# Two layers of a hybrid diffusion backbone: some output-projection rows take the second token set behind the norm, and three gate/up accumulators run k-tile by k-tile

## The chip, the cores and the metric

The kernel runs on one core of a Trainium2 chip. Its engines work side by side and wait for each other by semaphores: TensorE (PE, the matrix products, with its weight loads PEld), VectorE (DVE), ScalarE (ACT), GpSimd (POOL) and SyncE (SP, whose queue issues the DMA transfers). Each engine takes its own instructions strictly in the order in which they stand. The metric is the device time of one execution in microseconds, as the median of several runs.

## The reference

Two layers work on 512 latent tokens ("LAT") and 256 context tokens ("CTX") of width 1024. The second layer reads the context but updates only the latent tokens.

```python
for l in range(DEPTH):                       # DEPTH = 2
    need_ctx = l < DEPTH - 1
    h = modulate(rms_norm(x, g_mix[l]), mx[:, 0], mx[:, 1])
    # w_in, then three mixers: latent attention (MLA), neighbourhood attention, gated DeltaNet
    ...
    x = x + mx[:, 2] * (jnp.concatenate([mla_o, na_o, dn_o], axis=-1) @ w_out[l])
    h = modulate(rms_norm(x, g_ffn[l]), mx[:, 3], mx[:, 4])
    x = x + mx[:, 5] * swiglu(h, w_gate[l], w_up[l], w_down[l])
    if need_ctx:
        # the same two steps for ctx, with mc, mla_c, na_c, dn_c
        ...
return rms_norm(x, g_final)
```

## The kernel before

**Products.** Each fp32 matrix is split into a high and a low part in TensorE's fp32r type, and a product is made of three: high x high, high x low, low x high (`mm3`, and `gemm` at L343 to L350, which runs over k-tiles). All activations lie transposed: 128 channels on the partitions, tokens as columns. A matmul takes at most 512 columns, so LAT is one matmul and CTX a matmul of 256.

**Weights.** `wtiles` (L206 to L218) loads a weight tile by SP into `wr` (two buffers), casts it on ScalarE into the high part (`wh`, or `kh` for a slot of its own), and subtracts on GpSimd to get the low part (`wl`, `kl`). `wr` is free again when the subtraction has read it; `wh` and `wl` have two buffers each.

**Output projection** (L1240 to L1298). The token sets of layer 0 are LAT and CTX. In layer 1 there is only LAT; it is one set for the first part and two halves of 256 columns (`HALVES`) for the second. The first part (`acc_o`) runs over eight row tiles m: a weight tile of `w_out` (128 x 768), then for each token set 18 matmuls (six k-tiles, three products each) over the DeltaNet and neighbourhood outputs. VectorE adds the result into `xT` (L1273). The second part (`acc_o2`) takes the remaining two k-tiles, those of latent attention, with six matmuls for each m, and loops over token sets first and then m. As soon as the first set has all its m, `rstd_of` (L268 to L291) makes its norm: ScalarE squares (`nacc`, `nsq`), VectorE and GpSimd add them up, two PE products with a matrix of ones (`ms`) sum over partitions, and ScalarE makes Ln and Exp (`nrs`). The second set's `acc_o2` follows and is PE's work during that chain.

**Accumulators.** PSUM has 8 banks. In layer 0 `acc_l` is one bank of 512 columns, `acc_c` one of 256, and `acc_b` gives three of 512 and two of 256. `acc_c` serves the context's `acc_o`, and its `acc_o2` of every third m.

**Gate and up projection** (L1305 to L1345). `norm_mod` (L293 to L306) makes one k-tile of the normed input: VectorE multiplies (`nt`, two buffers), ScalarE adds the shift and rounds (`fh`), VectorE makes the low part (`fl`). The first tiles of `w_gu` begin on the first token set while its k-tiles come in (`first`, two accumulators; each a `gemm` of its own), and take the second token set later. The FFN's accumulators `acc_gu` (1024 columns, four buffers) reuse the banks of the output projection as these come free.

**Order.** A tile scheduler puts each engine's instructions in order from its own estimate of the times. So the order of the code says only what depends on what, and a small edit moves rows far behind it.

Of the kernel before, what the change touches and what calls it, by code (L numbers as in the profile page):

```python
# [17 lines left out]
P = 128  # L18
D = 1024
KD = D // P  # L20
# [5 lines left out]
LAT = slice(0, TL)  # L26
HALVES = (slice(0, TL // 2), slice(TL // 2, TL))
CTX = slice(TL, T)
# [18 lines left out]
INV = ((4, 3), (4, 3))  # L47
WV = ((6,), (23,))
MR = 2
MLA_ENG = ["GGVVGVGGV", "GGVGVVVGV"]  # L50
TILE_KV, TILE_QL, TILE_AB, TILE_K, TILE_V, TILE_Q, TILE_NK, TILE_NQ, TILE_Z = 0, 1, 3, 4, 8, 12, 16, 18, 20
HS = [slice(h * P, (h + 1) * P) for h in range(4)]
# [48 lines left out]


def mm(nc, out, lhsT, rhs, start=True, stop=True):
    nc.tensor.matmul(out, lhsT, rhs, start=start, stop=stop)  # L104


def mm3(nc, out, l, r, start=True, stop=True):
# [18 lines left out]
def emit(ctx, tc, a, out, dbg=None):  # L126
    nc = tc.nc
# [213 lines left out]
    def gemm(acc, wh, wl, xh, xl, sts, c0=0):  # L341

        nk = len(xh)  # L343
        for st in sts:
            for k in range(nk):
                w = slice(k * P, (k + 1) * P)
                o = acc[:, st.start - c0:st.stop - c0]
                mm(nc, o, wh[:, w], xh[k][:, st], k == 0, False)
                mm(nc, o, wh[:, w], xl[k][:, st], False, False)
                mm(nc, o, wl[:, w], xh[k][:, st], False, k == nk - 1)  # L350


    es_x = ExitStack()
# [9 lines left out]
def layer(tc, nc, a, l, es_x, xT, env, nx):  # L363
# [900 lines left out]
    def out_proj(nm, m, st_, s, w, mh, ml):  # L1264
        n = st_.stop - st_.start
        if nm == "acc_o":
            acc = (acc_l if st_ == LAT else acc_c)(nm)
        elif st_ in HALVES:
            acc = acc_l(nm)[:, 0:n] if m % 8 in (0, 1) else acc_b(nm, 512)[:, 0:n] if m % 8 < 5 else acc_c(nm) if m % 8 == 5 else acc_b(nm, n)
        else:  # L1270
            acc = (acc_l if st_ == LAT else acc_c)(nm) if m % (BO[n] + 1) == 0 else acc_b(nm, n)
        gemm(acc, *w, mh, ml, (st_,), st_.start)
        stt(out=xT[:, m, st_], in0=acc, scalar=mod[l][:, 2, m, s:s + 1], in1=xT[:, m, st_], op0=ALU.mult, op1=ALU.add)  # L1273
# [8 lines left out]
            tt(out=mxl[:, :, tok], in0=qT[:, :, tok], in1=mxh[:, :, tok].bitcast(F32), op=ALU.subtract)  # L1282
    m6 = [(mxh[:, i], mxl[:, i]) for i in range(4)] + [load_split(mp, i) for i in (2, 3)]
    m0 = load_split(mp, 0)
    for m in range(KD):
        w = wtiles(a["w_out"][l, m], 6 * P)
        for s, st_ in enumerate(sts):
            out_proj("acc_o", m, st_, s, w, *zip(*m6))

    wb = [wtiles(a["w_out2"][l, i], 1024, mp, 2) for i in range(2)]  # L1290
    segs, es_r = sts if need_ctx else HALVES, ExitStack()
    sb = pool(es_r, f"sb_fn{l}", 2, side=A_)
    for st_ in segs:
        for m in range(KD):
            c = (m % 4) * 2 * P
            out_proj("acc_o2", m, st_, int(st_ == CTX), [w[:, c:c + 2 * P] for w in wb[m // 4]], *zip(m0, m1))
        if st_ == segs[0]:
            rs = e.rstd_of(xT, lambda nm: acc_b(nm, 512), sb, (st_,))[0]  # L1298
    es_m.close()
    es_kq.close()  # L1300
    es_p.close()
# [5 lines left out]
    with ExitStack() as es:  # L1307
# [2 lines left out]
        es_f = ExitStack()  # L1310
        hp = pool(es_f, f"hf{l}", side=B_)
        hh, hl = [[hp.tile([P, T], F32R, name=f"f{x}{k}") for k in range(KD)] for x in "hl"]
        first, es_g = [], ExitStack()
        sg = pool(es_g, f"gu{l}", side=B_)
        for cols in segs:
            if cols == segs[1]:

                for j in range(2):
                    first.append((wtiles(a["w_gu"][l, 0, j], 1024), b2("acc_gu")))
                    gemm(first[j][1], *first[j][0], hh, hl, segs[:1])  # L1320
                rs = e.rstd_of(xT, b2, sb, (cols,))[0]
            for k in range(KD):
                e.norm_mod(xT, l, 1, sb, hh, hl, k, cols, rs)
        second = [wtiles(a["w_gu"][l, 1, j], 1024, sg, 2) for j in range(2)]
        es_r.close()
        es_a.close()
        ap_ = pool(es, f"act{l}", side=A_)
# [4 lines left out]
        for (t0, t1) in FFN_PARTS:  # L1332
            ah, al = [], []
            for t in range(t0, t1):
                accs = []
                for j in range(2):
                    w, acc = (wtiles(a["w_gu"][l, t, j], 1024) if t > 1 else second[j], b2("acc_gu")) if t else first[j]
                    gemm(acc, *w, hh, hl, sts if t else segs[1:])
                    if t == 1 and j == 1:
                        es_g.close()  # L1340
                    accs.append(acc)
                    if t > 0:
                        next(ada, None)
                av = sb.tile([P, T], F32, tag="av", name="av", bufs=2)
                silu = S.activation(out=av[:, :nT], in_=accs[0][:, :nT], func=AF.Silu)  # L1345
                if t == FFN_PARTS[-1][1] - 1:
                    e.preload(silu)
                tt(out=av[:, :nT], in0=accs[1][:, :nT], in1=av[:, :nT], op=ALU.mult)  # L1348
                h_ = ap_.tile([P, T], F32R, tag="ah", name="ah", bufs=8)
                l_ = ap_.tile([P, T], F32R, tag="al", name="al", bufs=8)  # L1350
                S.copy(out=h_[:, :nT], in_=av[:, :nT])  # L1351
                after.append(tt(out=l_[:, :nT], in0=av[:, :nT], in1=h_[:, :nT].bitcast(F32), op=ALU.subtract))  # L1352
                ah.append(h_)
                al.append(l_)
# [112 lines left out]
```

## Time and profile before

| what | value |
| --- | --- |
| median of 3 runs | 2119.75 us (2119.36 to 2120.94) |
| profiled execution | 2125.45 us, span 2123.6 us |
| mean granted TensorE clock | 0.968 |
| PE busy | 1990.2 us (94%) |
| DVE busy | 1172.3 us (55%) |
| POOL busy | 758.7 us (36%) |
| ACT busy | 714.3 us (34%) |

The span runs from the first to the last instruction of the profiled execution; its whole time and the median of the other runs stand beside it. The granted clock is a share of 2.4 GHz; the chip gives 2.4 or 1.2 GHz, and a mean between them says how long each was given. Matmuls overlap in their pipeline, so the distance of two starts says more than the duration of one. The profile's page lists the busy shares; the trace's timeline lists each instruction with the idle time before it and what ended that.

### The profile page before, as it was taken

Reading aid. Unit: us, or ns where it says so; the run is one execution under the profiler, and the core shown is the slowest. Engines: PE = TensorE matmul, PEld = TensorE weight load, DVE = VectorE, ACT = ScalarE, POOL = GpSimd, SP = SyncE. Lnnn points to the kernel's source line nnn. Section 1 sums busy time; section 2 is a strip of 40 time slices with the busy share of each in tenths; the row PEclk is TensorE's granted clock in tenths of the full one; section 3 lists DMA queues with packets and bytes.
Section 4 is the critical chain, followed back from the end, with each engine's and each line's share of the span. In section 5 each row is a group of like instructions: output and inputs, shape, how many; then the busy total and the mean of one; then the engine's idle time right before and its main releaser. Section 6 shows DMA issues by size and latency. Waiting matters only on the chain. (4 is left out here: it accounts for less than half of the span.)

```text
span 2123.6 us, 32023 instructions
## 1 busy us (share of the span) xinstructions
PE 1990.2 (94%) x12770; PEld 1684.4 (79%) x12770; DVE 1172.3 (55%) x2045; ACT 714.3 (34%) x1385; POOL 758.7 (36%) x540
## 2 busy tenths in 40 slices
PE   6999998998998999999999988888998889999998
PEld 4788787887787888888888876767787678888887
DVE  4888813667656457246443268894568753212123
ACT  5433322334544221122122244333434543222233
POOL 3466132104322222322222443823311353444444
PEclk9999998999999999999999999999999999999999
DMA  7324252543322345344442331334232231333332
GB/s 279 82 76 153 81 157 77 168 149 112 104 64 78 109 126 165 97 130 131 128 129 76 121 95 55 119 120 124 91 88 77 87 95 60 99 99 94 95 97 92
DMA packets 119309, 232.56 MB, mean 110 GB/s; under 512 B 30516, under 2 KB 55988, under 8 KB 119032
## 3 DMA queue, kind: packets, MB, share of 16 engines
q1 hardware_dynamic: 119160, 230.51, 34.9%
q8 instruction: 101, 1.65, 0.3%
q14 instruction: 48, 0.39, 0.1%
HBM read 199.46 MB, written 31.01 MB: 109 GB/s over the span
## 5 line engine op out<-in xcount | busy, mean ns | idle before, releaser
L217 POOL TENSOR_TENSOR wl<-wr,wh 128x1024 fp32r<-128x1024 f32 (+2 forms) x188 | 442.0, 2352 | 848.4 <-ACT wh L216 834.9
L216 ACT CAST wh<-wr 128x1024 fp32r<-128x1024 f32 (+2 forms) x190 | 193.5, 1019 | 713.0 <-PE acc_gu L104 287.6
L104 PE MATMUL acc_gu<-fh,wh 128*128 128x512 f32 (+1 forms) x1024 | 359.1, 353 | 9.5 <-ACT fh L304 8.7
L104 PE MATMUL acc_gu<-fl,wh 128*128 128x512 f32 (+1 forms) x1024 | 361.0, 353 | 4.1 <-DVE fl L305 4.1
L104 PE MATMUL acc_gu<-fh,wl 128*128 128x512 f32 (+1 forms) x1024 | 360.2, 352 | 0.0
L104 PE MATMUL acc_in<-hh,wh 128*128 128x512 f32 (+1 forms) x640 | 230.5, 364 | 18.6 <-ACT xp L491 6.9
L104 PE MATMUL acc_in<-hl,wh 128*128 128x512 f32 (+1 forms) x640 | 229.9, 360 | 3.2 <-DVE hl L305 2.0
L104 PE MATMUL acc_in<-hh,wl 128*128 128x512 f32 (+1 forms) x640 | 227.3, 359 | 3.4 <-POOL wl L217 3.4
L104 PEld LDWEIGHTS acc_gu<-fh,wh 128*128 128x128 f32 x1024 | 194.1, 190 | 37.5 <-ACT fh L304 10.9
L1348 DVE TENSOR_TENSOR av<-acc_gu,av 128x768 f32<-128x768 f32 (+1 forms) x44 | 36.3, 825 | 338.4 <-PE acc_gu L104 330.0
L104 PEld LDWEIGHTS acc_gu<-fl,wh 128*128 128x128 f32 x1024 | 195.0, 190 | 30.3 <-DVE fl L305 4.3
L104 PEld LDWEIGHTS acc_gu<-fh,wl 128*128 128x128 f32 x1024 | 194.9, 190 | 26.3
L104 PEld LDWEIGHTS acc_in<-hh,wh 128*128 128x128 f32 x640 | 126.1, 198 | 45.4 <-ACT xp L491 8.6
L104 PE MATMUL acc_d<-al,wh 128*128 128x512 f32 (+1 forms) x444 | 157.2, 354 | 0.0
L104 PE MATMUL acc_d<-ah,wh 128*128 128x512 f32 (+1 forms) x444 | 157.2, 354 | 0.0
L104 PE MATMUL acc_d<-ah,wl 128*128 128x512 f32 (+1 forms) x444 | 156.1, 354 | 0.0
L254 DVE CUSTOM_DVE_ANT_0 junk<-wada,scb 128x1024 f32<-128x1024 f32 x112 | 145.3, 1297 | 6.8 <-DMA wada<-w_adaT 4.0
L104 PEld LDWEIGHTS acc_in<-hl,wh 128*128 128x128 f32 x640 | 127.0, 198 | 25.2 <-DVE hl L305 4.6
L104 PEld LDWEIGHTS acc_in<-hh,wl 128*128 128x128 f32 x640 | 126.1, 198 | 22.8 <-POOL wl L217 4.7
L1366 DVE SCALAR_TENSOR_TENSOR xT<-acc_d,mod,xT 128x512 f32<-128x512 f32 (+1 forms) x76 | 46.5, 634 | 155.2 <-PE acc_d L104 155.2
L501 DVE SCALAR_TENSOR_TENSOR cy<-xp,cw,cy 128x770 f32<-128x770 f32 (+1 forms) x96 | 117.7, 1226 | 20.5 <-ACT cy L499 18.5
L1352 DVE TENSOR_TENSOR al<-av,ah 128x768 fp32r<-128x768 f32 (+1 forms) x44 | 100.4, 2282 | 35.1 <-ACT ah L1351 35.1
(391 smaller groups left out, 3857.0 us busy)
## 6 DMA issues: line engine op xcount, KB each, us to landing
wr<-w_gu SPq DMA_DIRECT2D x88, 512.0 KB, 3.5
wada<-w_adaT SPq DMA_DIRECT2D x56, 512.0 KB, 3.4
wr<-w_in SPq DMA_DIRECT2D x48, 512.0 KB, 3.6
wr<-w_dn SPq DMA_DIRECT2D x32, 448.0 KB, 3.3
wada<-w_ada SPq DMA_DIRECT2D x24, 512.0 KB, 3.4
wada<-w_ada SPq DMA_DIRECT2D x8, 1024.0 KB, 8.1
wr<-w_dn SPq DMA_DIRECT2D x16, 512.0 KB, 3.5
xT<-xT SPq DMA_DIRECT2D x16, 384.0 KB, 4.9
```

The source lines that it names most:

```text
L104: nc.tensor.matmul(out, lhsT, rhs, start=start, stop=stop)
L216: S.copy(out=hi[:, sl], in_=raw[:, sl])
L217: eng.tensor_tensor(out=lo[:, sl], in0=raw[:, sl], in1=hi[:, sl].bitcast(F32), op=ALU.subtract)
L254: V.tensor_tensor_reduce(out=junk, in0=w, in1=scb[:, s], scale=1.0, scalar=0.0, op0=ALU.mult, op1=ALU.add, accum_out=mod[l][:, part, j, s: ...
L501: stt(out=y[:, :wid], in0=xp[:, j:j + wid], scalar=w_(j), in1=y[:, :wid], op0=ALU.mult, op1=ALU.add)
L1348: tt(out=av[:, :nT], in0=accs[1][:, :nT], in1=av[:, :nT], op=ALU.mult)
L1352: after.append(tt(out=l_[:, :nT], in0=av[:, :nT], in1=h_[:, :nT].bitcast(F32), op=ALU.subtract))
L1366: stt(out=xT[:, m, st_], in0=acc, scalar=mod[l][:, 5, m, s:s + 1], in1=xT[:, m, st_], op0=ALU.mult, op1=ALU.add)
```

## The change

Row tiles m = 5, 6, 7 in layer 0 and m = 6, 7 in layer 1 (`BEHIND`) compute `acc_o` at first for the first token set only. Behind the first set's `rstd_of` the same m are computed for the second set (CTX in layer 0, the second half in layer 1). Their weights are loaded, cast and subtracted a second time, and their matmuls are issued no earlier than the last `acc_o2` matmul of the first set (`tc.issue_after`). In layer 1 the blocks m = 6, 7 become two blocks of 256 columns in place of one of 512.

`first` now has three accumulators (gate 0, up 0 and gate 1, the last with weights in a slot of its own), whose weights are loaded before the norm loop. One loop over k-tiles gives each k-tile to the three in turn. The third used to be `second[0]`; in layer 1 it used to take both halves as one set of 512 columns and now takes two of 256.

```diff
+BEHIND = ((5, 6, 7), (6, 7))
...
-                mm(nc, o, wl[:, w], xh[k][:, st], False, k == nk - 1)
+                last["mm"] = mm(nc, o, wl[:, w], xh[k][:, st], False, k == nk - 1)
...
-            acc = (acc_l if st_ == LAT else acc_c)(nm)
+            acc = acc_c(nm) if st_ == CTX else acc_l(nm)[:, 0:n]
...
+    segs = sts if need_ctx else HALVES
     for m in range(KD):
         w = wtiles(a["w_out"][l, m], 6 * P)
-        for s, st_ in enumerate(sts):
+
+        for s, st_ in enumerate(segs[:1] if m in BEHIND[l] else sts):
             out_proj("acc_o", m, st_, s, w, *zip(*m6))
...
             rs = e.rstd_of(xT, lambda nm: acc_b(nm, 512), sb, (st_,))[0]
+            behind = e.last["mm"].ins
+            for m in BEHIND[l]:
+                w = wtiles(a["w_out"][l, m], 6 * P)
+                with tc.issue_after(behind):
+                    out_proj("acc_o", m, segs[1], int(segs[1] == CTX), w, *zip(*m6))
...
-        first, es_g = [], ExitStack()
+        es_g = ExitStack()
         sg = pool(es_g, f"gu{l}", side=B_)
+        first = [(wtiles(a["w_gu"][l, t, j], 1024, *((sg, 2) if t else ())), b2("acc_gu")) for t, j in ((0, 0), (0, 1), (1, 0))]
         for cols in segs:
             if cols == segs[1]:
 
-                for j in range(2):
-                    first.append((wtiles(a["w_gu"][l, 0, j], 1024), b2("acc_gu")))
-                    gemm(first[j][1], *first[j][0], hh, hl, segs[:1])
+                for k in range(KD):
+                    w_ = slice(k * P, (k + 1) * P)
+                    for (wh, wl), acc in first:
+                        mm3(nc, acc[:, segs[0]], (wh[:, w_], wl[:, w_]), (hh[k][:, segs[0]], hl[k][:, segs[0]]), k == 0, k == KD - 1)
                 rs = e.rstd_of(xT, b2, sb, (cols,))[0]
...
-        second = [wtiles(a["w_gu"][l, 1, j], 1024, sg, 2) for j in range(2)]
+        second = wtiles(a["w_gu"][l, 1, 1], 1024, sg, 2)
...
-                    w, acc = (wtiles(a["w_gu"][l, t, j], 1024) if t > 1 else second[j], b2("acc_gu")) if t else first[j]
-                    gemm(acc, *w, hh, hl, sts if t else segs[1:])
+                    i = 2 * t + j
+                    w, acc = first[i] if i < 3 else (wtiles(a["w_gu"][l, t, j], 1024) if i > 3 else second, b2("acc_gu"))
+                    gemm(acc, *w, hh, hl, sts if i > 2 else segs[1:])
```

The change moves rows on every engine. First VectorE in layer 0 where the norm of the latent tokens begins, before. `nt` and `fl` are the norm's k-tiles; `xT<-acc_o2_...` with 256 columns is the addition of a context result.

```order
825 L1273 SCALAR_TENSOR_TENSOR xT_6078<-acc_o2_6653,mod0_88,xT_6078 128x256
826 L279 TENSOR_TENSOR nacc1_6787<-nacc1_6787,nsq_6805 128x256
827 L297 SCALAR_TENSOR_TENSOR nt_6692<-xT_6078,gs0_90,nrs_6594 128x512
828 L297 SCALAR_TENSOR_TENSOR nt_6696<-xT_6078,gs0_90,nrs_6594 128x512
829 L305 SCALAR_TENSOR_TENSOR fl0_6681<-nt_6692,mod0_88,fh0_6673 128x512
830 L305 SCALAR_TENSOR_TENSOR fl1_6682<-nt_6696,mod0_88,fh1_6674 128x512
831 L297 SCALAR_TENSOR_TENSOR nt_6700<-xT_6078,gs0_90,nrs_6594 128x512
832 L297 SCALAR_TENSOR_TENSOR nt_6704<-xT_6078,gs0_90,nrs_6594 128x512
833 L305 SCALAR_TENSOR_TENSOR fl2_6683<-nt_6700,mod0_88,fh2_6675 128x512
```

The last context addition stands ahead of the first `nt`. The same place on VectorE in the changed kernel; `acc_o_6569` and `acc_o_6595` are the context blocks of m = 6 and 7, `acc_o2_6615` and `acc_o2_6639` those of m = 0 and 3, all four in the bank of `acc_c`:

```order
818 L299 SCALAR_TENSOR_TENSOR nt_6731<-xT_6078,gs0_90,nrs_6534 128x512
819 L299 SCALAR_TENSOR_TENSOR nt_6735<-xT_6078,gs0_90,nrs_6534 128x512
820 L1275 SCALAR_TENSOR_TENSOR xT_6078<-acc_o_6569,mod0_88,xT_6078 128x256
821 L1275 SCALAR_TENSOR_TENSOR xT_6078<-acc_o_6595,mod0_88,xT_6078 128x256
822 L307 SCALAR_TENSOR_TENSOR fl0_6699<-nt_6731,mod0_88,fh0_6691 128x512
823 L1275 SCALAR_TENSOR_TENSOR xT_6078<-acc_o2_6671,mod0_88,xT_6078 128x256
824 L307 SCALAR_TENSOR_TENSOR fl1_6700<-nt_6735,mod0_88,fh1_6692 128x512
825 L299 SCALAR_TENSOR_TENSOR nt_6739<-xT_6078,gs0_90,nrs_6534 128x512
826 L1275 SCALAR_TENSOR_TENSOR xT_6078<-acc_o2_6615,mod0_88,xT_6078 128x256
827 L299 SCALAR_TENSOR_TENSOR nt_6743<-xT_6078,gs0_90,nrs_6534 128x512
828 L307 SCALAR_TENSOR_TENSOR fl2_6701<-nt_6739,mod0_88,fh2_6693 128x512
829 L1275 SCALAR_TENSOR_TENSOR xT_6078<-acc_o2_6639,mod0_88,xT_6078 128x256
```

The context additions now stand between the norm's k-tiles, one every two or three rows. ScalarE at the same place of layer 0, before; `nrs` are Ln and Exp, `kh` the casts of two gate/up weight tiles:

```order
469 L216 CAST kh_6847<-wr_6846 128x1024
470 L216 CAST kh_6853<-wr_6852 128x1024
471 L278 ACTIVATE nsq_6805<-xT_6078 128x256
472 L288 ACTIVATE nrs_6594<-ms_6591,eps_64 128x512
473 L289 ACTIVATE nrs_6594<-nrs_6594 128x512
474 L304 ACTIVATE fh0_6673<-nt_6692,mod0_88 128x512
475 L304 ACTIVATE fh1_6674<-nt_6696,mod0_88 128x512
476 L304 ACTIVATE fh2_6675<-nt_6700,mod0_88 128x512
```

And in the changed kernel, where `wh_6590` is the weight tile of m = 7, `wh_6711` and `wh_6718` those of the first two gate/up tiles:

```order
464 L218 CAST wh_6590<-wr_6589 128x768
465 L280 ACTIVATE nsq_6845<-xT_6078 128x256
466 L290 ACTIVATE nrs_6534<-ms_6531,eps_64 128x512
467 L291 ACTIVATE nrs_6534<-nrs_6534 128x512
468 L218 CAST wh_6711<-wr_6710 128x1024
469 L306 ACTIVATE fh0_6691<-nt_6731,mod0_88 128x512
470 L306 ACTIVATE fh1_6692<-nt_6735,mod0_88 128x512
471 L218 CAST wh_6718<-wr_6717 128x1024
472 L306 ACTIVATE fh2_6693<-nt_6739,mod0_88 128x512
```

Two casts went from ahead of Ln to behind Exp and between the `fh`, and they use the buffers that m = 6 and m = 7 read from. The same engine in layer 1, before, from Ln to the first k-tiles of the norm (the row numbers are those of the whole program):

```order
987 L288 ACTIVATE nrs_15959<-ms_15956,eps_64 128x256
988 L289 ACTIVATE nrs_15959<-nrs_15959 128x256
989 L278 ACTIVATE nsq_16155<-xT_15607 128x256
990 L304 ACTIVATE fh0_16038<-nt_16057,mod1_89 128x256
991 L304 ACTIVATE fh1_16039<-nt_16061,mod1_89 128x256
992 L216 CAST kh_16212<-wr_16211 128x1024
993 L216 CAST kh_16218<-wr_16217 128x1024
```

And in the changed kernel, where `wh_16135` and `kh_16142` are the weights of the second and the third gate/up tile:

```order
990 L291 ACTIVATE nrs_15977<-nrs_15977 128x256
991 L280 ACTIVATE nsq_16256<-xT_15625 128x256
992 L280 ACTIVATE nsq_16259<-xT_15625 128x256
993 L280 ACTIVATE nsq_16265<-xT_15625 128x256
994 L218 CAST wh_16135<-wr_16134 128x1024
995 L277 ACTIVATE nacc0_16252<-xT_15625 128x256
996 L280 ACTIVATE nsq_16262<-xT_15625 128x256
997 L218 CAST kh_16142<-wr_16141 128x1024
998 L306 ACTIVATE fh0_16108<-nt_16148,mod1_89 128x256
```

Two weight casts stand ahead of `fh0` where there was none. Elsewhere, too, rows moved: in layer 1 the scheduler orders the DeltaNet and the attention otherwise from the loads onward.

## Rows read from the trace of the kernel before

**Rows 1.** Stretches: length, busy PE, PEld, DVE, ACT, POOL (count), clock, DMA share, GB/s.

```profile
660.00:680.00 20.00, 13.35 (x50) 10.05 (x49) 17.07 (x24) 11.19 (x19) 6.42 (x4) 0.74 0.40 135
1600.00:1720.00 120.00, 107.73 (x739) 87.99 (x739) 84.60 (x184) 54.19 (x157) 34.58 (x39) 0.97 0.27 80
```

**Rows 2.** Timeline, PE, layer 0: start, duration, operation, [idle before, what ended it].

```profile
657.77 0.28 PE L104 MATMUL acc_o<-mh,kh 128*128 128x256 f32 x1
657.88 0.28 PE L104 MATMUL acc_o<-ml,kh 128*128 128x256 f32 x1
...
669.89 1.22 PE L104 MATMUL acc_gu<-fh,wh 128*128 128x512 f32 x2 [6.65 <-ACT fh L304]
...
673.46 0.63 PE L104 MATMUL acc_gu<-fh,wl 128*128 128x512 f32 x1
673.89 0.63 PE L104 MATMUL acc_gu<-fh,wh 128*128 128x512 f32 x1
...
675.58 0.40 PE L104 MATMUL acc_gu<-fl,kh 128*128 128x512 f32 x1
675.81 0.40 PE L104 MATMUL acc_gu<-fh,kl 128*128 128x512 f32 x1
```

**Rows 3.** Timeline of ACT, DVE and POOL in the same gap.

```profile
662.60 1.98 ACT L216 CAST kh<-wr 128x1024 fp32r<-128x1024 f32 x2
...
665.50 0.63 ACT L289 ACTIVATE nrs<-nrs 128x512 f32<-128x512 f32 x1
669.11 1.39 ACT L304 ACTIVATE fh<-nt,mod 128x512 fp32r<-128x512 f32 x2 [2.98 <-DVE nt L297]
...
661.70 0.48 DVE L1273 SCALAR_TENSOR_TENSOR xT<-acc_o,mod,xT 128x256 f32<-128x256 f32 x1 [0.48 <-PE acc_o L104]
...
666.25 3.48 DVE L297 SCALAR_TENSOR_TENSOR nt<-xT,gs,nrs 128x512 f32<-128x512 f32 x2
...
673.53 0.75 DVE L297 SCALAR_TENSOR_TENSOR nt<-xT,gs,nrs 128x512 f32<-128x512 f32 x1
674.20 0.75 DVE L305 SCALAR_TENSOR_TENSOR fl<-nt,mod,fh 128x512 fp32r<-128x512 f32 x1
...
663.71 4.82 POOL L217 TENSOR_TENSOR kl<-wr,kh 128x1024 fp32r<-128x1024 f32 x2
```

**Rows 4.** Timeline of POOL and DVE: an addition from PSUM beside a subtraction.

```profile
643.11 2.37 POOL L217 TENSOR_TENSOR wl<-wr,wh 128x1024 fp32r<-128x1024 f32 x1 [7.68 <-ACT wh L216]
...
643.82 0.75 DVE L1273 SCALAR_TENSOR_TENSOR xT<-acc_o,mod,xT 128x512 f32<-128x512 f32 x1 [0.83 <-PE acc_o L104]
```

**Rows 5.** Timeline of PE at the same place in layer 1.

```profile
1740.59 0.47 PE L104 MATMUL acc_gu<-fh,wh 128*128 128x256 f32 x2 [0.81 <-DVE xT L1273]
...
1743.78 0.50 PE L104 MATMUL acc_gu<-fh,wh 128*128 128x256 f32 x2 [1.43 <-ACT fh L304]
1748.40 0.58 PE L104 MATMUL acc_gu<-fl,wh 128*128 128x256 f32 x1 [4.12 <-DVE fl L305]
...
1749.00 0.41 PE L104 MATMUL acc_gu<-fh,wh 128*128 128x256 f32 x1
1749.21 0.41 PE L104 MATMUL acc_gu<-fl,wh 128*128 128x256 f32 x1
...
1756.81 0.50 PE L104 MATMUL acc_gu<-fh,wh 128*128 128x256 f32 x2 [0.64 <-ACT fh L304]
```

**Rows 6.** Timeline of DVE and POOL in layer 1, first two in that gap.

```profile
1744.06 3.43 DVE L279 TENSOR_TENSOR nacc<-nacc,nsq 128x256 f32<-128x256 f32 x2
...
1741.21 5.12 POOL L217 TENSOR_TENSOR kl<-wr,kh 128x1024 fp32r<-128x1024 f32 x2 [0.97 <-ACT kh L216]
...
1717.74 1.84 POOL L217 TENSOR_TENSOR wl<-wr,wh 128x768 fp32r<-128x768 f32 x1 [2.89 <-ACT wh L216]
```

**Rows 7.** Timeline of PE at the end of layer 0's attention.

```profile
647.65 0.39 PE L104 MATMUL acc_o<-m1h,kh 128*128 128x256 f32 x1 [0.36 <-ACT m1h L1228]
```

**Rows 8.** DMA issues: count, KB each, median us from issue to landing.

```profile
wr<-w_gu SPq DMA_DIRECT2D x88, 512.0 KB, 3.5
```

More of the change, by code (lines that the diff above doesn't have):

```diff
@@ L103, in mm @@
 def mm(nc, out, lhsT, rhs, start=True, stop=True):
-    nc.tensor.matmul(out, lhsT, rhs, start=start, stop=stop)
+    return nc.tensor.matmul(out, lhsT, rhs, start=start, stop=stop)
 def mm3(nc, out, l, r, start=True, stop=True):
@@ L1284, in layer @@
     m0 = load_split(mp, 0)
+    segs = sts if need_ctx else HALVES
     for m in range(KD):
         w = wtiles(a["w_out"][l, m], 6 * P)
-        for s, st_ in enumerate(sts):
+        for s, st_ in enumerate(segs[:1] if m in BEHIND[l] else sts):
             out_proj("acc_o", m, st_, s, w, *zip(*m6))
     wb = [wtiles(a["w_out2"][l, i], 1024, mp, 2) for i in range(2)]
-    segs, es_r = sts if need_ctx else HALVES, ExitStack()
+    es_r = ExitStack()
     sb = pool(es_r, f"sb_fn{l}", 2, side=A_)
```

## The prediction

> **What bounds the kernel now.** I read the page first: its slices show TensorE (PE) busy nearly throughout, and no other engine near that. A change can therefore win only where PE stands still or runs at its lower clock. The busy times by stretch show where: from 660 to 680 us PE is busy 13.35 of 20 us at a granted clock of 0.74 [rows 1], which mixes its two levels, 2.4 and 1.2 GHz. That is one of the two places that this change touches.
>
> Layer 0, read from the timeline [rows 2]. The last 512-wide product of the latent tokens ends at 657.77; 30 products of 256 columns for the context tokens follow at 0.12 us each (657.77, 657.88), with the sums of squares (`ms`) between. Then PE waits 6.65 us for ScalarE's `fh`, and its next nine products have a pitch of 0.43 instead of 0.23 us until 675.58. From 657.77 to 675.58 are 17.8 us. Work in it: 30 x 0.12 + 0.9 for `ms` (four passes of 512) + 9 x 0.23 + 0.5 for the second `ms` (four of 256) = 7.1. The gap costs **10.7 us**, of which some 3 are the lower clock.
>
> What ends last there [rows 3]: behind the last `ms` ScalarE makes two weight casts (662.60, 1.98 us), then Ln and Exp until 666.13; VectorE (DVE) then needs 3.48 us for two `nt` of which one alone takes 0.75, while GpSimd (POOL) subtracts two weight tiles (663.71, 4.82 us); `fh` starts at 669.11. An addition into `xT` from PSUM took its usual 0.75 us beside such a subtraction [rows 4]. So the rows say that what stretches is the DVE operations with both tensors in SBUF (`nt`, `fl`, the sums), not `xT`.
>
> Layer 1 has the same place with 256-wide halves: waits of 0.81, 1.43, 4.12 and 0.64 us and a pitch of 0.21 instead of 0.12 for 22 products (about 2 us) [rows 5]: some **9.5 us**. There two sums took 3.43 us while POOL subtracted (1741.21, 5.12 us) [rows 6]. Both gaps together, 20 us or 1%, are the stake.
>
> **The change part by part.** The profiled execution took 2125.45 us, 5.7 above the median of 2119.75; I make the sum as a difference, which goes for both, and give the time against the median.
>
> *Extra work.* Five `w_out` tiles come twice: five loads of 384 KB, five casts, five POOL subtractions (1.84 us each [rows 6]). The loads go through SP's queue among the other weights, and the DMA engines were busy 0.40 of the stretch [rows 1], so layer 0 hides them; the casts and subtractions are counted in the walks below. PE gets no more columns, but in layer 1 two blocks of 18 products of 512 become 36 of 256, and the third gate/up tile's 24 become 48: 60 more instructions. Two of 256 take 0.24 against 0.23, so 60 x 0.01 = **+0.6 us**.
>
> *Layer 0, behind the norm.* Let L be the end of the last latent product. The 54 products (m = 5, 6, 7 for the context) now stand behind L, and cover 54 x 0.12 = 6.5 us more; if everything else stayed, the wait of 6.65 would be gone. It doesn't stay. By the order, the three `acc_o` blocks, the context's `acc_o2` of m = 0, 3, 6 and later the second gate/up tile use one PSUM bank in turn, each waiting for the `xT` addition that empties it; and these additions now stand on DVE between `nt` and `fl`, where before there was none. I walk along the order with the durations of [rows 2, 3] (`nt`, `fl`, 0.75, `xT` of 256 0.48, `fh` 0.7, a cast 1.0, a subtraction 2.4 or 1.84), in us after L:
> - PE: m=5 to 2.2, two `acc_o2` to 3.6, `ms` to 4.1, m=6 to 6.3, one `acc_o2` to 7.0. ScalarE: Ln and Exp to 5.8, since the two casts no longer stand ahead. DVE: `nt0`, `nt1` to 7.25, only then the `xT` of m=6 (7.7). So m=7 starts at 7.8 (wait 0.8) and ends at 9.95.
> - ScalarE's cast of the second gate/up tile needs the buffer that m=7 reads: 10.05 to 11.05. POOL subtracts from 11.2 to 13.6. DVE stands with `fl1` and `nt2` before the `xT` that empties the bank; `fl1` has both tensors in SBUF and waits until 13.6. That `xT` ends at 15.5, and the next `acc_o2` of the bank starts at 15.6 instead of 11.3 (wait 4.3).
> - The next waits for `nt3`, `fl2` and `xT`: 17.45 (wait 1.2), ends 18.15. The first gate/up tile starts, three products to 18.85. The second needs the last `xT`, behind `nt4`, `fl3`, a sum, `nt5`, `fl4`: 21.0, or 23.3 if POOL's next subtraction starts before `fl4`.
>
> Dense from 21.0 to 23.3, with 90 x 0.12 + 0.9 + 3 x 0.23 = 12.4 of work: 8.7 to 10.9 us lost, and 0 to 3.1 by the lower clock (the wait is now in pieces; [rows 2] show only what one long piece does). Against 10.7 that is -2.0 to +3.3; I take **+0.6**, the middle.
>
> Whether the pieces cost the lower clock is the open half of it. In the rows it fell behind one wait of 6.65 us. The Trainium skill, "TensorE: Matmul & The Clock Gate", section "What's actually happening", says that the low clock is the default and that activity releases it. By that rule PE, which works between the pieces, could stay at 2.4 GHz, and layer 0 would come out at the lower end, -2.0, the whole at 2120; no row here shows pieces of 1 to 4 us.
>
> *The attention's tail in layer 0.* These 54 products filled the waits between the last attention tiles. There `m1h` ended a wait of only 0.36 us [rows 7]; three blocks remain as fillers for three tiles. Bounds: 0 (the rest is enough) and 3 us (an estimate: 1 us for each of three tiles, about three times the wait of the row); I take **+1.5**.
>
> *Layer 1.* Its 36 products behind the norm and 24 of the third tile give cover, (36 + 24) x 0.12 = 7.2 us. But a w_gu load takes 3.5 us from issue to landing [rows 8], there are two `wr` buffers, and each is free only after POOL's subtraction; two `w_out` tiles now go first. Walking along: the cast of the first gate/up tile at 5.7 after the last product of the first half, of the second 9.2 (behind m=7), of the third 12.7; this third cast stands ahead of `fh0` on ScalarE, so `fh0` ends at 14.2 where PE is ready at 11.2 (wait 3.0). POOL's subtraction then holds `fl0` (2.1), the next one `nt4` (2.0); small ones 1.3; and before L, 1.5 for the second `w_out2` tile, since m = 6, 7 take half the time. About 9.9, with 0 to 2 of lower clock, against 9.5. If the loads come early enough for the third cast not to wait, 3 to 4 us less. Bounds -4 and +2.4; I take **0**.
>
> *Layer 0's third accumulator* changes nothing: before, a third gate/up tile is already interleaved there. *The order of attention in layer 1* is different throughout, with the DeltaNet output ready later and `acc_o` then in one run. No row prices it: that stretch, 1600 to 1720 us, had PE busy 107.7 of 120 us [rows 1], so it lost 12. I take 0, and half of that either way, -6 to +6, as bounds.
>
> Sum: 0.6 + 0.6 + 1.5 + 0 + 0 = +2.7: 2119.75 + 2.7 = **2122**.
>
> **The rivals.**
> - *A, the wait moves (forecast).* As walked: 2122, 2115 to 2127.
> - *B, the cover works.* DVE empties the bank in time, or POOL's subtraction falls between its operations: layer 0 then loses 10.7 - 2.4 (subtraction) - 2.2 (second tile) - 3.1 (clock) = 3, 7.7 less; layer 1 gains the 4 of its bound; +2.1 for split and tail: 2119.75 - 9.6 = 2110. For it: the wait before is one long chain and 6.5 us of work lies under it. Against: the bank.
> - *C, slower.* The same bank chain, but POOL's next subtraction also starts just before `fl4` (23.3 instead of 21.0), and the clock falls in both gaps: 3.3 + 3 (tail) + 2.4 + 0.6 = +9.3: 2129. It decides at the moment at which the cast of the third tile ends, 19.9 by the walk, against the 19.8 at which `fl4` comes up: a tenth of a microsecond. For it: two sums took 3.43 us that way [rows 6]. The Trainium skill, "SBUF — State Buffer", section "SBUF: two separate sides", states it as a rule: DVE and GpSimd share a port pair as an exclusive lock, whoever starts first keeps it for the whole instruction, and a DVE operation with two SBUF inputs needs it. By that rule the later one always pays in full, and this rival's 2129 stands or falls with who is first.
> - *D, layer 1's other order decides*, up to 6 us either way: 2116 to 2128.
>
> **How the numbers follow.** 0.2% (4.2 us) is about what a measurement can tell from no change. A 0.45 (of it 0.28 within 0.2%, 0.17 slower); B 0.28, faster; C 0.20, slower; D 0.07 (0.03, 0.01, 0.03). Faster 0.31, same 0.29, slower 0.40. The likeliest is A. The range reaches into B and C: 2109 to 2131.
>
> **What would show it.** In the profile after: PE waits for DVE `xT` in front of `acc_o2` and the second `acc_gu` in layer 0, a wait of about 4 us among them that lies under a POOL subtraction; no wait of 6 us for `fh`; in layer 1 the first `acc_gu` waits for `fh` behind a cast that a DMA released. If these waits are under 1 us each and PE's clock stays at 1.00 from 660 to 680, B is right and the bank was harmless. The forecast is wrong too if busy PE time in layer 1's attention changes by more than these gaps.

## The result and the profile after

The changed kernel takes 2138.93 us (median of 4 runs, 2136.44 to 2144.49) against 2120.35 (4 runs, 2119.36 to 2121.02) of the kernel before: a ratio of 1.0093, interval 1.0078 to 1.0109. It is slower by 18.6 us, where 2.7 were forecast, and lies above the range.

The profiled execution of after took 2144.49 us (span 2142.5), that of before 2125.45 (span 2123.6). First the page of after, its part on busy time and the slices of the granted clock; then the whole span as one stretch, first of before and then of after (columns as in [rows 1]).

```profile
PE 2015.2 (94%) x12830; PEld 1703.8 (80%) x12830; DVE 1178.8 (55%) x2047; ACT 717.5 (33%) x1390; POOL 771.6 (36%) x545
...
PEclk9899998999998999999999999989879999999999
```

```profile
0.00:2123.50 2123.50, 1990.24 (x12770) 1684.41 (x12770) 1172.28 (x2045) 714.26 (x1385) 758.70 (x540) 0.97 0.35 110
```

```profile
0.00:2142.40 2142.40, 2015.15 (x12830) 1703.80 (x12830) 1178.81 (x2047) 717.48 (x1390) 771.58 (x545) 0.96 0.35 109
```

The reader is to see two things. PE has the 60 instructions more that the splitting brings, as worked out. And its idle time **fell**, from 2123.5 - 1990.24 = 133.3 us to 2142.4 - 2015.15 = 127.3, while the kernel became longer: busy time grew by 25 us with no column added to it. What grew is the time at the lower clock. With two levels, 2.4 and 1.2 GHz, a mean granted clock m over a span s means 2(1 - m)s at the lower one: 2 x 0.032 x 2123.6 = 136 us before, 2 x 0.042 x 2142.5 = 180 after, 44 more. A stretch in which PE alone sets the pace does at least half its work at 1.2 GHz, so these 44 are worth at most 22 us.

Where it happened is read from stretches bounded by the same instructions in each trace. The first fence is before, the second after. The first row of each is layer 0 from the end of DeltaNet to the first `acc_d`, the second layer 1 from its first `acc_in` (the input projection) to its first `acc_gu`, called its attention here, and the third from there to the first `acc_d`.

```profile
518.80:807.00 288.20, 276.79 (x1694) 235.08 (x1693) 169.40 (x321) 105.49 (x224) 80.05 (x51) 0.97 0.30 96
...
1225.70:1740.60 514.90, 461.60 (x3295) 383.53 (x3293) 354.94 (x676) 211.35 (x468) 196.60 (x177) 0.95 0.32 95
1740.60:1838.90 98.30, 92.11 (x436) 78.01 (x437) 38.83 (x47) 33.38 (x52) 37.89 (x17) 0.97 0.25 76
```

```profile
514.50:809.30 294.80, 282.37 (x1693) 237.65 (x1692) 173.86 (x321) 107.70 (x230) 87.57 (x54) 0.96 0.30 98
1228.00:1763.60 535.60, 484.23 (x3330) 402.74 (x3328) 358.41 (x677) 213.56 (x472) 201.51 (x179) 0.91 0.30 91
1763.60:1857.90 94.30, 92.32 (x461) 79.29 (x462) 38.93 (x47) 32.44 (x50) 38.49 (x18) 0.96 0.29 86
```

Layer 0 lost 294.8 - 288.2 = 6.6 us; layer 1's attention 535.6 - 514.9 = 20.7; layer 1's gate/up won 4.0. Together +23.3, against 2144.49 - 2120.35 = 24.1 of this execution over the median of before. (The spans differ by 18.9 only, since in the profile of before DeltaNet ended 4.3 us later, 518.8 against 514.5, before anything that the change touches runs.) So most of the loss lies in a stretch whose work the change doesn't name: layer 1's attention.

**Layer 0.** The timeline of PE behind the norm in after, which answers to [rows 2]; the last latent product is shown, every row with a wait, and the product at which the pitch is back at 0.23 us. The profile leaves numbers out of names, so its `acc_o` is also `acc_o2`.

```profile
649.78 0.39 PE L106 MATMUL acc_o<-m1h,kl 128*128 128x512 f32 x1
...
658.86 0.36 PE L106 MATMUL acc_o<-mxh,wh 128*128 128x256 f32 x1 [0.52 <-DVE xT L1275]
...
661.83 0.39 PE L106 MATMUL acc_o<-mh,kh 128*128 128x256 f32 x1 [0.58 <-DVE xT L1275]
...
666.35 0.58 PE L106 MATMUL acc_o<-mh,kh 128*128 128x256 f32 x1 [3.54 <-DVE xT L1275]
...
668.57 0.58 PE L106 MATMUL acc_o<-mh,kh 128*128 128x256 f32 x1 [0.58 <-DVE xT L1275]
...
672.42 0.76 PE L106 MATMUL acc_gu<-fh,wh 128*128 128x512 f32 x1 [0.92 <-DVE xT L1275]
...
677.62 0.40 PE L106 MATMUL acc_gu<-fl,wh 128*128 128x512 f32 x1
```

The timeline of DVE and POOL at the longest of these waits, which answers to [rows 3].

```profile
661.69 0.74 DVE L307 SCALAR_TENSOR_TENSOR fl<-nt,mod,fh 128x512 fp32r<-128x512 f32 x1
...
662.74 2.49 DVE L307 SCALAR_TENSOR_TENSOR fl<-nt,mod,fh 128x512 fp32r<-128x512 f32 x1
665.16 0.74 DVE L299 SCALAR_TENSOR_TENSOR nt<-xT,gs,nrs 128x512 f32<-128x512 f32 x1
665.82 0.47 DVE L1275 SCALAR_TENSOR_TENSOR xT<-acc_o,mod,xT 128x256 f32<-128x256 f32 x1
...
662.34 2.34 POOL L219 TENSOR_TENSOR wl<-wr,wh 128x1024 fp32r<-128x1024 f32 x1 [1.27 <-ACT wh L218]
```

The wait of 6.65 us for `fh` is gone. In its place stand five waits for DVE's `xT` in front of `acc_o` and the second `acc_gu`, 6.1 us together; the longest, 3.54, is there because `fl`, which takes 0.74 alone, took 2.49 beside POOL's subtraction, with an `nt` and the `xT` that empties the bank queued behind it. After that wait PE is at the lower clock until 677.62. From L = 650.0, the end of the last latent product, to there are 27.6 us for 90 x 0.12 + 0.9 + 15 x 0.23 = 15.2 of work: 12.5 lost, against 10.7 before [rows 2].

**Layer 1.** Eighty microseconds of its attention, first of before, then of after.

```profile
1520.00:1600.00 80.00, 74.80 (x886) 65.72 (x882) 55.13 (x135) 31.35 (x87) 23.12 (x19) 0.96 0.33 100
```

```profile
1520.00:1600.00 80.00, 78.34 (x722) 66.90 (x722) 46.26 (x127) 24.93 (x75) 17.46 (x15) 0.72 0.23 70
1540.00:1560.00 20.00, 20.00 (x128) 16.35 (x126) 8.51 (x27) 4.99 (x15) 1.04 (x1) 0.50 0.13 41
1560.00:1580.00 20.00, 20.00 (x167) 18.61 (x168) 9.04 (x25) 4.13 (x14) 1.04 (x1) 0.53 0.18 53
```

PE is busy for more of it (78.3 of 80 us against 74.8), yet issues 722 instructions instead of 886. Its clock is at 0.50 from about 1534 to 1579, although its longest wait there is 0.20 us. In this stretch 2 x (0.28 - 0.04) x 80 = 38 us more than before are at the lower clock, 38 of the 44, worth at most 19 of the 20.7 us.

### The profile page after: what moved, and what is told of

The parts are those of the page before. It is cut to its first block, busy times and chain, and to the rows that moved or that the text cites. A ratio compares the mean times of both kernels' runs of the same rounds, so it can differ in the third digit from the quotient of the medians.

```text
span 2142.5 us, 32188 instructions
## 1 busy us (share of the span) xinstructions
PE 2015.2 (94%) x12830; PEld 1703.8 (80%) x12830; DVE 1178.8 (55%) x2047; ACT 717.5 (33%) x1390; POOL 771.6 (36%) x545
## 5 line engine op out<-in xcount | busy, mean ns | idle before, releaser
L219 POOL TENSOR_TENSOR wl<-wr,wh 128x1024 fp32r<-128x1024 f32 (+2 forms) x193 | 451.0, 2337 | 826.3 <-ACT wh L218 818.2
L503 DVE SCALAR_TENSOR_TENSOR cy<-xp,cw,cy 128x770 f32<-128x770 f32 (+1 forms) x96 | 122.8, 1279 | 24.0 <-ACT cy L501 20.5
```

What stands on the lines that cost most here:

```text
L219: eng.tensor_tensor(out=lo[:, sl], in0=raw[:, sl], in1=hi[:, sl].bitcast(F32), op=ALU.subtract)
L503: stt(out=y[:, :wid], in0=xp[:, j:j + wid], scalar=w_(j), in1=y[:, :wid], op0=ALU.mult, op1=ALU.add)
```

## Experiments

Times are medians with the kernel before run beside them on the same chip. The table gives two stretches from one profile of each kernel: layer 0 (end of DeltaNet to first `acc_d`), layer 1 (first `acc_in` to first `acc_gu`) with its time at the lower clock, and the ratio of the whole. The low-clock column is summed from the granted clock that the trace records. A profile is one execution, and the time at the lower clock differs from one to the next; the ratio is that of several runs.

| kernel | layer 0, us | layer 1, us | of it low clock | whole, ratio and interval |
|---|---|---|---|---|
| before | 288.2 | 514.9 | 51 | |
| after | 294.8 | 535.6 | 96 | 1.0093 [1.0078, 1.0109] |
| again | 295.2 | 527.9 | 68 | 1.0078 [1.0051, 1.0105] |
| l0_behind_gu | 292.0 | 540.9 | 99 | 1.0104 [1.0080, 1.0128] |
| l1_behind_gu | 288.0 | 518.6 | 58 | 1.0001 [0.9990, 1.0013] |
| gu_only | 288.3 | 517.2 | 58 | 0.9990 [0.9977, 1.0003] |
| burst16 | 295.4 | 528.2 | 68 | 1.0091 [1.0078, 1.0104] |
| narrow128 | 294.9 | 546.4 | 109 | 1.0154 [1.0141, 1.0167] |
| bank | 289.2 | 531.5 | 72 | 1.0062 [1.0038, 1.0086] |
| behind_only | 293.9 | 520.7 | 55 | 1.0053 [1.0040, 1.0066] |
| b_67 | 291.5 | 514.5 | 51 | 1.0012 [1.0002, 1.0022] |
| p24 | 287.0 | 528.4 | 79 | 1.0056 [1.0044, 1.0068] |
| bbank_7 | 291.5 | 513.9 | 61 | 1.0005 [0.9995, 1.0016] |
| gu_only2 | 288.1 | 515.8 | 61 | 0.9985 [0.9974, 0.9996] |

**The same program again.** No edit.

> The changed kernel once more, unedited. In its first profile PE was busy throughout from 1534 to 1579 us while the granted clock stood at 0.50; the low clock over the whole span came to 179 us against 136 before, and half of the difference, 21.6 us, is more than the whole loss of 18.6. Theory (the low clock in the attention and DeltaNet stretch of layer 1 is the loss): the time is 12 to 24 us above before, and a stretch at 0.50 with PE busy stands again somewhere between 1500 and 1700 us, its length differing from run to run. Rival (a disturbance of that one execution): the clock stands at 1.00 there and the time is within 6 us of before.

2137.82 us (2129.33 to 2148.53, 7 runs; before 2121.53, 24 runs). One program spreads over 19 us, and the spans follow the clock: 2127.5 us at a mean of 0.970, 2136.5 at 0.965, 2146.5 at 0.958. By 2(1 - m)s that is 128, 150 and 180 us at the lower clock, so a microsecond of it costs (2146.5 - 2127.5) / (180 - 128) = 0.37 us. The profiled run shows the same stretch, with the clock back sooner:

```profile
1540.00:1560.00 20.00, 20.00 (x190) 16.98 (x189) 11.26 (x37) 7.07 (x24) 2.08 (x2) 0.83 0.30 88
1560.00:1580.00 20.00, 20.00 (x302) 17.86 (x301) 15.38 (x44) 8.44 (x27) 2.69 (x4) 1.00 0.17 47
```

Eight products of `sp` take 2.08 us at the lower level and 1.16 at the upper; the timeline of PE shows them, and one group of `o_na`, in after (first fence) and in this run.

```profile
1535.70 2.08 PE L106 MATMUL sp<-w,kt 128*128 128x128 f32 x8 [0.20 <-DVE w L1037]
...
1544.31 1.98 PE L106 MATMUL o_na<-pt,nav 128*64 128x128 f32 x16
...
1549.54 2.08 PE L106 MATMUL sp<-w,kt 128*128 128x128 f32 x8
```

```profile
1537.30 2.08 PE L106 MATMUL sp<-w,kt 128*128 128x128 f32 x8 [0.53 <-DVE w L1037]
...
1545.90 1.54 PE L106 MATMUL o_na<-pt,nav 128*64 128x128 f32 x16
...
1549.36 1.16 PE L106 MATMUL sp<-w,kt 128*128 128x128 f32 x8
```

Up to there the two runs issue the same instructions, 1.6 us apart. In one the clock comes back within the `o_na` at 1545.90, some 10 us after the fall; in the other PE works on at 1.2 GHz for some 34 us longer. So the loss in layer 1 has a part that varies from run to run; but even the fastest of the seven, at the 128 us that before also shows (118 to 145 in its runs), is some 8 us over before.

**The halves of the change.**

```diff
-BEHIND = ((5, 6, 7), (6, 7))
+BEHIND = ((5, 6, 7), ())    # l0_behind_gu
+BEHIND = ((), (6, 7))       # l1_behind_gu
+BEHIND = ((), ())           # gu_only
```

> BEHIND only in layer 0, with the three gate/up accumulators. Its order on every engine is that of the changed kernel up to the end of layer 1's attention. Theory (layer 1's other order, which layer 0's rows bring about, and the low clock in it): as slow as the changed kernel, 10 to 24 us above before, with the long stretch at 0.50. Rival (the split blocks and second weight loads in layer 1 cost the time): within 4 us of before.

> BEHIND only in layer 1, with the three gate/up accumulators. The order on VectorE and ScalarE is that of the kernel before until the end of layer 1's attention. Theory (layer 1's other order): within 4 us of before, no stretch of over 15 us at 0.50. Rival (the blocks in layer 1): 8 us or more above before.

> BEHIND empty in both layers: only the three gate/up accumulators. VectorE and SyncE keep exactly the order of the kernel before. Theory: within 4 us of before (in layer 1 24 products of 512 become 48 of 256, +0.2 us, and the third accumulator gives 2.9 us of work to the norm of the first half). Rival (the k-tile loop over three accumulators costs): 4 us or more above.

2145.29, 2121.35 and 2120.80 us. The late rows of **layer 0**, with the three accumulators, bring the whole loss, and they bring most of it in **layer 1** (540.9 us against 514.9), where this kernel leaves the rows as they were. The late rows of layer 1 are worth nothing either way: the stretch from the last `s_mla` to the first `acc_gu` grows from 39.5 to 43.4 us, and gate/up behind it shrinks from 98.3 to 94.0; 2.8 of this are the three accumulators' own (95.5 in gu_only), which alone are no loss. One expectation was missed: l1_behind_gu has a stretch of 17 us at 0.50, 1522 to 1539, where at most 15 were expected.

**Is it the lower clock, and what ends it?** Extra products in the middle of the low stretch, 16 wide ones in one kernel, 128 small ones in the other. Their result is written over by the product that follows.

```diff
+                    if l == 1 and (pair, qt, j) == (1, 0, 1):
+                        for _ in range(16):                                    # burst16
+                            mm(nc, s_, qh[:, 0:P], qh[:, LAT])
+                        for _ in range(128):                                   # narrow128
+                            mm(nc, s_[0:32, 0:32], qh[0:32, 0:32], qh[0:32, 0:32])
```

> The changed kernel with 16 products of 128x128 by 512 columns, whose result nothing reads, put ahead of one score tile of the neighbourhood attention in layer 1, right behind the place where the clock fell in both profiles (the second head of pair 1, first query tile). They cost 16 x 0.23 = 3.7 us of PE at 2.4 GHz, 6.9 at 1.2. Theory (in that order the low clock lasts, over work in small tiles, until something wide comes): the clock is back at 1.00 within some 10 us of the burst, the low time over the whole span falls from a median of 150 us and more to under 140, and the time is 2126 to 2134 in spite of the extra work. Rival (the clock's length there has nothing to do with what PE does): the low time stays at 128 to 180 and the time rises by 4 us, to 2140 and more.

> The same place with 128 products of 32x32 by 32 columns instead, which keep PE busy for about as long (some 3.4 us at the 26 ns from start to start of the 32x32 products in the trace) and do little in the array. Theory: as slow as the changed kernel or slower, 2134 to 2148, with low times of 130 to 185 us. Rival (any extra work there, or the other order behind it, breaks the low stretch): as fast as the run with wide products.

2140.28 us (2135.37 to 2142.94) and 2153.15 (2151.91 to 2153.87), 13 us apart. Eighty microseconds of burst16, then of narrow128, and the rows of two such groups.

```profile
1520.00:1600.00 80.00, 77.55 (x885) 66.51 (x883) 53.85 (x139) 29.57 (x85) 22.39 (x18) 0.96 0.31 95
```

```profile
1520.00:1600.00 80.00, 77.91 (x778) 67.01 (x777) 43.78 (x123) 24.07 (x73) 16.54 (x14) 0.72 0.22 70
```

```profile
1539.34 3.61 PE L106 MATMUL s_na<-nqh 128*128 128x512 f32 x8
```

```profile
1550.51 2.74 PE L106 MATMUL s_na<-nqh 32*32 32x32 f32 x48
```

Eight wide products took 3.61 us, 48 small ones 2.74, so either addition is some 5 to 7 us of PE's time. Behind the first eight wide ones the clock stood at 1.00, behind the small ones at 0.50 until about 1580, as long as in after, which has none of them. In the whole span the four runs of narrow128 have 176 to 189 us at the lower clock, those of burst16 141 to 158: some 33 less in the mean. That is 13 / 33 = 0.39 us for each, near the 0.37 of again, so the price of the lower clock holds here too. That a burst **helps** is not shown: 2140.28 is no less than after's, the unedited program shows 128 to 180, as little as burst16, and in again the clock came back in the same place without a burst. Both expectations were missed, 2126 to 2134 with wide products and 2134 to 2148 with small ones.

**The bank in layer 0.** The late rows take the two small PSUM banks of `acc_b` in place of the one of `acc_c`.

```diff
-            acc = acc_c(nm) if st_ == CTX else acc_l(nm)[:, 0:n]
+            acc = (acc_b(nm, n) if m in BEHIND[l] else acc_c(nm)) if st_ == CTX else acc_l(nm)[:, 0:n]
```

> The changed kernel, but the context blocks of m = 5, 6, 7 in layer 0 use the two small banks of acc_b and not the one of acc_c. Theory (the bank with its xT additions between nt and fl makes the waits in layer 0 of 0.5, 0.6, 3.5, 0.6 and 0.9 us): the waits for xT in front of acc_o2 and of the second acc_gu shrink to under 2 us in sum, and the stretch from the end of layer 0's DeltaNet to the first acc_d is 3 to 6 us shorter; the whole stays above before by what layer 1 loses. Rival (POOL's subtraction is what holds): the long wait of 3.5 us stays within 1 us.

2130.66 us (2127.62 to 2146.88). Layer 0 is at 289.2, 5.6 less than in after. All waits of PE that are left from 645 to 690:

```profile
666.15 0.38 PE L106 MATMUL acc_o<-mh,kh 128*128 128x256 f32 x1 [1.41 <-DVE xT L1275]
668.74 0.58 PE L106 MATMUL acc_o<-mh,kh 128*128 128x256 f32 x1 [1.61 <-DVE xT L1275]
```

Two waits in place of five, 3.0 us in place of 6.1 (under 2 were expected): both stand in front of `acc_o2`, as the context's blocks still share three banks. From L to the first `acc_d` bank takes 154.9 us with 96 context products, after 159.3 with 90, before 149.2 with 30. By 0.12 us for each product that is a gain of 2.2 in bank where after lost 2.9: the single bank was what cost layer 0 behind its norm, with 3.1 us of waits and some 7 us more at the lower clock (14 in after behind L, 7 in bank). The 3.2 us that bank lost ahead of L remain. Layer 1 still loses 16.6 us.

**The late rows without the three accumulators**, then only as many as leave layer 1's order alone. Both take the edits of `BEHIND` and `out_proj` from the change, and gate/up as before.

```diff
+BEHIND = ((5, 6, 7), (6, 7))   # behind_only
+BEHIND = ((6, 7), ())          # b_67
```

> BEHIND in both layers, the gate/up accumulators as before. Theory (layer 0's BEHIND changes the order of layer 1 and that is what costs): 5 to 25 us above before. Rival (the three accumulators together with BEHIND cost): within 4 us of before.

> BEHIND only in layer 0 and only m = 6, 7, the gate/up accumulators as before. On every engine the order of layer 1 from its input projection to its attention is, row for row, that of the kernel before. Theory (layer 1 loses by its order alone, layer 0 by the bank, the subtractions and the low clock): within 5 us of before, layer 1 unchanged within 2 us, layer 0 from the end of its DeltaNet to the first acc_d 0 to 5 us longer. Rival (context blocks behind the norm cost layer 1 something of their own, whatever its order): 8 us or more above before.

2130.95 and 2123.97 us. In b_67 the scheduler puts layer 1's instructions in the order of before, row for row, and layer 1 takes 514.5 us against 514.9; only layer 0's +3.3 is left (2.9 of it ahead of L). behind_only has another order again, and layer 1 loses 5.8 us, of which 3.5 stand where layer 1's own late rows now lie (last `s_mla` to first `acc_gu`: 43.0 against 39.5). So the late rows of layer 0 do nothing to layer 1 where the order stays, and another order needn't cost much. How much one costs isn't told by how far it is from that of before: nine in ten of layer 1's PE rows stand in its sequence in behind_only, but also in bank, which lost 16.6 us (two in three in after).

**Another order, and nothing of the change.** The kernel before, with 24 copies of eight columns on DVE in layer 0, read by nobody; they move the scheduler's clock, and layer 1 comes out in a different order.

```diff
+            if l == 0:
+                for _ in range(24):
+                    jk = sb.tile([P, 8], F32, tag="jk", name="jk", bufs=1)
+                    V.tensor_copy(out=jk, in_=xT[:, 0, 0:8])
```

> The kernel before with nothing of the change: 24 VectorE copies of 8 columns are added behind layer 0's first norm, some 2 us of VectorE. The scheduler then orders layer 1's DeltaNet and attention otherwise; six in ten of PE's rows there still stand in the sequence of before. Theory (any other order of layer 1 than that of before costs 8 us or more, so the loss is not the change's own work): 6 to 20 us above before, nearly all of it between layer 1's input projection and its first acc_gu. Rival (the order of the changed kernel is bad by itself, and others do as well as before): within 4 us of before.

2133.86 us (2127.68 to 2136.17; before 2120.37, 23 runs), 12 us slower by the ratio and 13.5 by the medians. Layer 0 doesn't lose (287.0); layer 1 does, with the work of before in it. First p24, then b_67:

```profile
1222.00:1750.40 528.40, 475.79 (x3294) 393.01 (x3293) 357.50 (x676) 211.87 (x468) 199.12 (x177) 0.93 0.31 92
```

```profile
1224.10:1738.60 514.50, 463.10 (x3295) 383.36 (x3293) 353.94 (x676) 211.55 (x468) 196.97 (x177) 0.95 0.32 95
```

The same instructions, to one or two of 3294; 52.6 us idle in p24 (51.4 in b_67); but 12.7 us more of busy PE, at 0.93 instead of 0.95. This is after's picture without the change: the order alone is enough.

**What is worth keeping.** One late row with the other bank (bbank_7: `BEHIND = ((7,), ())`, the edit of `bank`, gate/up as before), and gu_only once more.

> BEHIND only in layer 0 and only m = 7, its block in a bank of acc_b, the gate/up accumulators as before; layer 1 keeps the order of the kernel before row for row. Theory: the cover behind the norm grows by 18 x 0.12 = 2.2 us and no bank is waited for, so layer 0 gains 0 to 3 us and the time is 0 to 3 us below before. Rival (POOL's additional subtraction and DVE's row order take it back): 0 to 3 us above before.

> The kernel with only the three gate/up accumulators once more, unedited, since it came out 0.1% under before with an interval that holds 1. In its profile layer 1 from the first acc_gu to the first acc_d took 95.5 us against 98.3. Theory (the third accumulator is worth these 2.8 us in layer 1 and nothing else moves): 1 to 3 us below before. Rival (that was the low clock's luck): within 1 us.

2122.34 us (before 2120.37): no gain. Its layer 0 takes 3.3 us longer, 2.2 of them ahead of L. gu_only2 gave 2120.25 (12 runs) beside 2122.34 of before (17), 0.9985 [0.9974, 0.9996]; the first time 0.9990 [0.9977, 1.0003]. The gain stands where it should: first `acc_gu` to first `acc_d` 95.0 us against 98.3. It is the one version whose interval lies below 1, and only in the second of two comparisons: some 2 us, less than the 0.2% that a measurement can tell from no change. l1_behind_gu and bbank_7 can't be told from before either.

## Why the prediction was wrong

The step that failed is "*the order of attention in layer 1* ... I take 0, and half of that either way, -6 to +6, as bounds". It measured 20.7 us in the profile of after, 13.0 in again, 26.0 in l0_behind_gu. The bound came from PE's idle time, the 12 us of [rows 1], as if another order could only fill or open gaps. The same row holds the other half of the price: a clock of 0.97 over 120 us, that is, PE nearly always at 2.4 GHz. Had its 107.7 us of busy time run at 1.2 GHz, they would have become up to twice as long (eight `sp` took 2.08 us there and 1.16 at 2.4); a bound from there would have been tens of microseconds. The row was also too narrow: 1600 to 1720 is 120 us of a stretch of 515, and 38 of the 44 us that are new at the lower clock lie outside it, at 1520 to 1600. By the profiles 44 of after's 96 us at the lower clock are new (half is 22.2, the most that they can be worth, and idle fell by 1.9: 20.3 of 20.7); in again 17 are new (8.5, and 2.8 more idle: 11.3 of 13.0); in p24 27 (13.7, and 0.7 less idle: 13.0 of 13.5). The prediction did say what would refute it, a change of busy PE in layer 1's attention by more than the gaps; it rose from 461.6 to 484.2.

**Layer 0**, forecast +2.1 (0.6 behind the norm, 1.5 for the tail), measured +6.6 and +7.0, and +3.8 in l0_behind_gu. The mechanism was right: the chain of bank, `xT` and POOL's subtraction under `fl`, with a longest wait of 4.3 us by the walk and 3.54 on the chip, and no wait of 6 us for `fh`. The sizes were low. 60 more context products stand behind L (90, as in the walk, against the 30 of [rows 2]; the text counts the 54 of `acc_o`), 7.2 us of work. From L to the first `acc_d` are 159.3 us against 149.2, so 2.9 were lost: 1.8 up to the product at which the pitch is back (12.5 against 10.7, inside the bounds of -2.0 to +3.3), the rest behind it, with a wait of 0.56 for the second norm's `nrs`. The tail: L came 139.0 us behind the end of DeltaNet before and 135.5 after, so 7.2 us of products taken away shortened it by 3.5; 3.7 were lost, above the bound of 3, where 1.5 was taken. The waits that were forecast between the last attention tiles are there, in place of the one of 0.36 [rows 7]:

```profile
629.24 0.39 PE L106 MATMUL s_mla<-kh,qh 96*128 96x256 f32 x1 [0.90 <-ACT pr L1208]
...
631.21 0.84 PE L1219 MATMUL tp_mla<-cst,pr 128*128 128x128 f32 x6 [0.26 <-DVE pr L1215]
...
638.05 0.50 PE L106 MATMUL acc_o<-mh,kh 128*128 128x512 f32 x1 [0.27 <-DVE xT L1275]
```

They add 1.1 us, near the 1.5 that was taken. Of the rest a part goes with the clock: 9 us of the tail were at the lower level in after, 7 before. l0_behind_gu has the same order and the same three waits, 3 us at the lower level, and lost 1.5 in the tail. So the +3.8 to +7.0 of layer 0 are one order at different clocks; 1 to 2 us of the tail, which neither waits nor clock explain, were not traced.

Behind the norm the clock went the way of the upper end. After 3.54 us of waiting PE stayed at the lower level for 11 us, with waits of only 0.58 and 0.92 between. The rule of the Trainium skill, "TensorE: Matmul & The Clock Gate", section "What's actually happening", that activity releases the throttle, would have given the lower end; in this trace the clock was not back before these 11 us of work, and in layer 1 not before 44 us with no wait over 0.20.

**Layer 1's norm**, forecast 0: the sum was right, by other terms than the walk's, and so partly by luck. l1_behind_gu is at 1.0001, since the 4 us gained behind the first `acc_gu` had been spent ahead of it, where the walk put 1.5. The wait that the walk named is there, the first `acc_gu` behind `fh`, and `fh` behind a weight cast on ScalarE (PE, then two rows of ACT, in after):

```profile
1763.63 0.50 PE L106 MATMUL acc_gu<-fh,wh 128*128 128x256 f32 x2 [1.66 <-ACT fh L306]
```

```profile
1762.14 1.03 ACT L218 CAST kh<-wr 128x1024 fp32r<-128x1024 f32 x1
1763.08 0.91 ACT L306 ACTIVATE fh<-nt,mod 128x256 fp32r<-128x256 f32 x2
```

It took 1.66 us instead of 3.0, and no DMA released that cast: ScalarE came to it without a wait. The waits from there on are 3.6 in all, where before had 7.0 [rows 5] and the walk 9.9 with what it put ahead of L: the loss behind the norm was overrated. (By its own rows the gap before is 7.0 + 22 x 0.09 = 9.0, not 9.5; the sum is hardly touched.)

**The rest.** Layer 0's third accumulator costs nothing there: right (288.3 in gu_only). The 0.6 for splitting can't be told apart. Of the rivals, C had the sign, and for layer 0's gap and tail nearly the size (6.3 us, measured 6.6), but not by the race that it named: `fl4` started ahead of POOL's next subtraction, by 0.2 us, and kept its 0.74 (DVE and POOL, in after). Its share of layer 1's norm did not come. D had the place, with a bound too small by a factor of two to four.

```profile
671.13 0.74 DVE L307 SCALAR_TENSOR_TENSOR fl<-nt,mod,fh 128x512 fp32r<-128x512 f32 x1
...
671.32 5.28 POOL L219 TENSOR_TENSOR kl<-wr,kh 128x1024 fp32r<-128x1024 f32 x2 [2.32 <-ACT kh L218]
```

**What stays open.** Why the lower clock ends after some 10 us in one run and 44 in another of the same program. Near 1535 every profile shows such a stretch: 7 to 17 us in the six with the order of before, 10 and 44 in after's, 20 in p24; no run shows what sets its length. Of the 8 us by which after exceeds before at equal low-clock time, layer 0 has 4 to 7; the rest is somewhere in layer 1's order, and was not traced to an instruction.

## What to carry to other kernels

An edit in one place can re-plan a stretch far behind it where a scheduler sets the order; bound such a stretch by what PE's clock can cost there, not by its idle time alone. Before such a loss is put down to the edit, run a kernel that shifts the order and does nothing else (p24), and one that has the edit in the old order (b_67). And when work is moved under a wait, list the PSUM banks that it takes in turn and who empties them: PE may then wait for a bank to be emptied in place of the result that it waited for.

## What the runs showed that was not expected

- PE busy for 20.0 of 20 us at a granted clock of 0.50, for some 40 us on end, on products of 32x32, 64x64 and up to 128 by 256 columns; the same program came back to 1.00 after some 10 us in another run.
- At that place 128 products of 32x32x32 left the clock at 0.50 until about 1580, and the time at 2153 us; with 16 products of 128x128x512 it was back at 1.00 behind the first eight. One profile of each can't tell this from the spread of the unedited program.
- Twenty-four copies of eight columns that nobody reads made the kernel 12 to 13.5 us slower, through the order of a layer that they are not in.
